# A hybrid decoder layer on one core: the delta rule's outputs split where they are made and loaded as two operands, the second merge's first two tiles in chunk order, the mixer's last pair at a lower priority

## The chip, the core and the metric

One Trainium2 chip, one of its cores. The metric is the device time of one execution in microseconds, as the median of the runs. TensorE is called PE here, VectorE DVE, ScalarE ACT, GpSimd POOL, and SyncE SP; nearly all transfers are issued from SP's queue.

## What is computed

One layer for 1024 prompt tokens and 32 sample tokens, width 1024, in float32. Two branches read the same normalised input: stick-breaking attention (8 heads of 64) and a gated delta rule (4 heads of 128). They are merged through two gates and two projections, and a channel mixer follows:

```python
q_a, k_a, v_a, u, z, a, b, g_a, g_b = jnp.split(rmsnorm(x) @ w_in, ...)
o_a = sb_prompt(q_a, k_a, v_a, sb_bias)                    # stick-breaking attention
o_b, ssm_new = gdn_branch(short_conv(u), z, a, b, ...)     # gated delta rule, chunk by chunk
y_a, y_b = o_a @ w_pa, o_b @ w_pb
x = x + (sigmoid(g_a) * y_a + sigmoid(g_b) * y_b) @ w_o
x = x + square(relu(rmsnorm(x) @ w_up)) @ w_down
```

## The kernel before

Every dense product is made of three. A float32 operand is split into a rounded part `h` (an ACT copy into the type F32R) and the rest `l` (a DVE subtraction), and `dense()` (lines 134 to 139) adds `wh·xh`, `wh·xl` and `wl·xh` over the contraction's tiles into one PSUM bank. Each operand of PE must therefore exist as two tiles.

The order of instructions on each engine's queue is not written out by hand. It is laid down when the kernel is built, by a planner that gives each engine, among what it holds to be ready, the instruction with the highest priority. Priority is the place in the program; `tc.high_priority()` puts a block at the very front, `high_priority(offset=n)` moves it forward by `n` places (a negative `n` moves it back), and `tc.issue_after(x)` keeps a block's instructions behind `x` on the queue. On the chip each queue runs in that order, whatever is ready.

The work goes in stages. `gdn_head(h)` (head of the delta rule, four calls) makes one head's output: after the last chunk it loads the gate `z_d[h]` into `zl`, a tile of the tag "cgb" (one buffer, shared with `qe` of the next head), multiplies it with the transposed output (L585) and stores it from SP to `o_d[4 + h]` (L586). The tag "vb" (one buffer) holds `vb`, the scaled values of a head, which the chunk loop's first product reads (L551). The sample tokens' output `dot` is stored in the same way (L778).

From about 640 us to 850 us the attention's 64 blocks (`blks`) run through a pipeline. For each block PE makes scores, ACT the sigmoid, POOL the mask and `1 - s` (L961, L964), DVE a running product and a multiplication (L968, L969), PE transposes (L111) and the products with the values (L1006, L1020). `pipeline(x0, x1, fill)` spreads other work for PE between the blocks. For the blocks up to 34 that is the gates' projections (`pd_g`, stores L1073); for the blocks from 34 on it is the second merge's `o_B @ w_pb`: 32 steps `pb_step(j, c, first)`, one for each of 8 column tiles `j` and 4 token chunks `c` (256, 256, 256 and 288 tokens). A step is `dense4` of 12 matmuls on `obh[c]`, `obl[c]`, and a product with the stored gate `tb[j]` on DVE (L1174). The steps go tile by tile, so that the fourth step needs the fourth chunk.

Between the two parts of the pipeline the input's pools are closed (`xctx`) and others opened in their place: `tbp` for the gates, `z2p`, and `obp` for `obh`, `obl` and one of the staging tiles. The delta rule's outputs come in here. Chunk 0 was loaded ahead at L1111 into a tile `ofb0` of a pool that was already there; chunks 1 to 3 are loaded at L1153 into `z2p` and `obp`. ACT copies each chunk into `obh[c]` (L1155), and DVE subtracts into `obl[c]` (L1156), both under `high_priority()`. `mark` is the last of these loads, and the gates of the tiles from 2 on are loaded behind it (L1169).

The mixer's first stage works on pairs of row tiles. `up_products(w7, f, g)` makes seven products, combines them on DVE, takes relu and square of two pairs of rows on ACT (L1437, L1438), combines those on DVE in `combos` (L1364 to L1367) and stores the result from SP into `hc_d` (L1368). Its last call is `(f, g) = (15, 1)`. The second stage begins at once: its loads are issued from POOL (L1495, L1503), `weight_part` splits the weights on ACT and DVE (L1517, L1518; the first part under `high_priority()`), and `pw` is its first product. The result of the last pair is read only in the last of three groups of that stage.

## Time and profile before

| | us |
|---|---|
| median of 3 runs | 1700.03 |
| lowest and highest run | 1699.78, 1703.91 |
| the profiled execution | 1701.33 |
| its span, first to last instruction | 1699.6 |

The profile is of one execution. Its span is 1.7 us shorter than that execution's own time. Of the span, PE is busy 98%, DVE 69%, ACT 46% and POOL 13%. The page's chain of work gives 89% of the span to PE, 4% to DVE, 2% to DMA, and 1% each to POOL and ACT. To read it: idle time of PE is what can be saved, in the stage where it stands, and the rows say what ended it; a busy PE runs at the granted clock, which is 1.00 in most stretches and lower in a few.

### The profile page before, as it was taken

How to read it: one execution, taken by the hardware profiler on the slowest of the kernel's cores; microseconds unless marked ns; L12 is line 12 of the kernel's file. 1: busy time of each engine (PE TensorE's matmuls, PEld its weight loads, DVE VectorE, ACT ScalarE, POOL GpSimd, SP SyncE). 2: the span in 40 equal slices, each digit the busy share in tenths (PEclk: the TensorE clock that was granted, in tenths of full speed). 3: DMA queues.
4: the chain of work that ended last, by engine and by line, in shares of the span. 5: the costliest groups of instructions: out<-in, count | busy, mean ns of one | idle time of the engine just before them, and what ended most of it. 6: DMA issues, size and time to landing. Idle time of an engine off the chain costs nothing.

```text
span 1699.6 us, 34650 instructions
## 1 busy us (share of the span) xinstructions
PE 1665.5 (98%) x13934; PEld 1616.3 (95%) x13934; DVE 1170.7 (69%) x2335; ACT 778.5 (46%) x1548; POOL 220.7 (13%) x243
## 2 busy tenths in 40 slices
PE   7999999999999999999999999999999999999998
PEld 6999999999999799988999999999999999999998
DVE  6656676877325337789776578877777678688964
ACT  5453434343324225555433455644444564334455
POOL 1110111110004226565300000000000000000000
PEclk9999999999999999999999999999999999999999
DMA  5132233244538577895144545555443765442231
GB/s 182 38 119 81 70 95 104 74 124 129 159 90 240 156 194 180 203 237 178 42 130 144 166 134 159 155 161 162 140 140 117 270 210 190 151 158 97 96 114 78
DMA packets 260205, 240.86 MB, mean 142 GB/s; under 512 B 55906, under 2 KB 217795, under 8 KB 260044
## 3 DMA queue, kind: packets, MB, share of 16 engines
q1 hardware_dynamic: 255094, 227.90, 44.4%
q0 software_dynamic: 3200, 10.52, 2.1%
q8 instruction: 109, 1.79, 0.4%
q10 hardware_dynamic: 1750, 0.23, 0.1%
q14 instruction: 52, 0.43, 0.1%
HBM read 164.02 MB, written 74.58 MB: 140 GB/s over the span
## 4 chain that ended last, share of the span: by engine, by line
PE 89%; DVE 4%; issue 2%; DMA 2%; POOL 1%; ACT 1%; SPq 0%; DVEq 0%; POOLq 0%; ACTq 0%
PE pu L139 6%; PE pu L137 6%; PE pu L138 6%; PE pw L137 6%; PE pw L138 6%; PE pw L139 6%; PE pd_g L137 3%; PE pd_g L138 3%; PE pd_g L139 3%; PE wt L111 1%; PE px L138 1%; PE px L137 1%; PE px L139 1%; PE pd_uk L139 1%; PE po L1006 1%
## 5 line engine op out<-in xcount | busy, mean ns | idle before, releaser
L137 PE MATMUL pu<-Xh,uh 128*128 128x264 f32 x812 | 229.8, 284 | 0.5 <-ACT t L1426 0.5
L139 PE MATMUL pu<-Xh,ul 128*128 128x264 f32 x812 | 230.1, 285 | 0.0
L138 PE MATMUL pu<-Xl,uh 128*128 128x264 f32 x812 | 229.8, 283 | 0.0
L137 PE MATMUL pw<-hc,w 128*128 128x264 f32 x784 | 220.8, 285 | 2.8 <-ACT w L1517 2.4
L138 PE MATMUL pw<-hc,w 128*128 128x264 f32 x784 | 220.0, 286 | 0.0
L139 PE MATMUL pw<-hc,w 128*128 128x264 f32 x784 | 216.3, 286 | 0.0
L137 PEld LDWEIGHTS pu<-Xh,uh 128*128 128x128 f32 x812 | 153.2, 189 | 0.9 <-ACT t L1426 0.7
L138 PEld LDWEIGHTS pu<-Xl,uh 128*128 128x128 f32 x812 | 152.8, 188 | 0.0
L139 PEld LDWEIGHTS pu<-Xh,ul 128*128 128x128 f32 x812 | 152.1, 188 | 0.0
L137 PEld LDWEIGHTS pw<-hc,w 128*128 128x128 f32 x784 | 148.1, 189 | 3.2 <-ACT w L1517 2.6
L137 PE MATMUL pd_g<-xh,wh_g 128*128 128x256 f32 (+1 forms) x512 | 149.9, 293 | 0.0
L138 PE MATMUL pd_g<-xl,wh_g 128*128 128x256 f32 (+1 forms) x512 | 149.6, 292 | 0.0
L139 PE MATMUL pd_g<-xh,wl_g 128*128 128x256 f32 (+1 forms) x512 | 149.0, 291 | 0.0
L138 PEld LDWEIGHTS pw<-hc,w 128*128 128x128 f32 x784 | 147.1, 189 | 0.0
L139 PEld LDWEIGHTS pw<-hc,w 128*128 128x128 f32 x784 | 145.7, 190 | 0.0
L968 DVE TENSOR_TENSOR_SCAN pr<-am 128x127 f32<-128x127 f32 (+7 forms) x64 | 89.5, 1399 | 19.1 <-POOL am L964 15.7
L137 PEld LDWEIGHTS pd_g<-xh,wh_g 128*128 128x128 f32 x512 | 97.2, 190 | 3.2 <-issue 2.6
L138 PEld LDWEIGHTS pd_g<-xl,wh_g 128*128 128x128 f32 x512 | 97.3, 190 | 2.5 <-issue 2.1
L139 PEld LDWEIGHTS pd_g<-xh,wl_g 128*128 128x128 f32 x512 | 97.1, 190 | 2.1 <-issue 2.0
L1517 ACT ACTIVATE w<-a 128x512 fp32r<-128x512 f32 x84 | 46.6, 620 | 94.6 <-PE pw L139 88.2
L1490 ACT ACTIVATE hc<-hc 128x528 fp32r<-128x528 f32 x98 | 62.1, 644 | 28.8 <-DMA hc<-hc_d 26.8
L139 PE MATMUL px<-mh,wl_wo 128*128 128x264 f32 x256 | 72.5, 286 | 1.3 <-DVE wl_wo L1262 1.2
(582 smaller groups left out, 5014.8 us busy)
## 6 DMA issues: line engine op xcount, KB each, us to landing
hc_d<-t SPq DMA_DIRECT2D x27, 924.0 KB
hc<-hc_d SPq DMA_DIRECT2D x94, 264.0 KB
a<-in_w_down_dram SPq DMA_DIRECT2D x52, 256.0 KB
ws_c<-in_w_in_dram SPq DMA_DIRECT2D x16, 512.0 KB
ws_wo<-in_w_o_dram SPq DMA_DIRECT2D x32, 256.0 KB
ua<-in_w_up_dram SPq DMA_DIRECT2D x16, 512.0 KB
ub<-in_w_up_dram SPq DMA_DIRECT2D x16, 512.0 KB
gA_d<-gt SPq DMA_DIRECT2D x8, 528.0 KB
```

The lines of the kernel that those rows point to most:

```text
L111: return PE.transpose(out, in_, ident[:k, :k])
L137: PE.matmul(pt[:, :n], lhsT=wh[k], rhs=xh[k], start=(k == 0), stop=False)
L138: PE.matmul(pt[:, :n], lhsT=wh[k], rhs=xl[k], start=False, stop=False)
L139: PE.matmul(pt[:, :n], lhsT=wl[k], rhs=xh[k], start=False, stop=(k == nk - 1))
L968: V.tensor_tensor_scan(pr[:, n - 1:0:-1], am_r, am_r, 1.0, op0=ALU.mult, op1=ALU.bypass)
L1006: PE.matmul(po[64 * r:64 * r + 64, 0:P], lhsT=vn[:, b, rs], rhs=wts[hh, 2 * m + r][:, b * P:(b + 1) * P], start=(b == 0), stop=(b == 2 * m ...
L1490: S_.activation(tl[:, 0], tl[:, 1].bitcast(F32), AF.Copy)
L1517: S_.activation(tl[:, 0], src, AF.Copy)
```

## The change

Three edits. First, `gdn_head` splits its output where it is made: ACT copies `zl` into a new tile `zh` (tag "vb"), DVE subtracts, and two stores replace the one, into two new buffers `ob_d`. The same goes for the sample tokens' `dot` (its copy takes a buffer of the tag "dyt"). In the merge the four chunks of `obh` and `obl` are then loaded directly, eight loads from SP in place of four loads, four ACT copies and four DVE subtractions; the load ahead at L1111 and the staging tiles fall away, and the first two gates' loads stand behind chunk 0's.

Second, the first eight steps of `pb_step` go chunk by chunk over the tiles 0 and 1; the other 24 stay as they were.

Third, relu, square, combinations and store of the pair (15, 1) stand under `high_priority(offset=-600)`, 600 places further back.

```diff
--- before.py
+++ after.py
@@ -146,6 +146,7 @@
     xT_d, o_d, x1_d = spill("xT_d"), spill("o_d"), spill("x1_d")
     gA_d, gB_d = spill("gA_d"), spill("gB_d")
     z_d = dr.tile([GH, P, NP], F32, name="z_d")
+    ob_d = [dr.tile([GH, P, T], F32, name=f"ob{x}_d") for x in "hl"]
     q_d = [dr.tile([4, P, NP], F32, name=f"q{x}_d") for x in "hl"]
     k_d = [dr.tile([4, P, NP], F32, name=f"k{x}_d") for x in "hl"]
     v_d = dr.tile([4, P, NC, P], F32, name="v_d")
@@ -583,7 +584,11 @@
         for hf, pt in enumerate(tr8(on, f"o{h}", gtile)):
             sl = slice(hf * 512, hf * 512 + 512)
             V.scalar_tensor_tensor(zl[:, sl], zl[:, sl], gnw, pt, op0=ALU.mult, op1=ALU.mult)
-        SY.dma_start(o_d[4 + h, :, 0:NP], zl)
+        zh = gk.tile([P, NP], F32R, tag="vb", name=f"zh{h}")
+        S_.activation(zh, zl, AF.Copy)
+        V.tensor_tensor(zl, zl, zh.bitcast(F32), op=ALU.subtract)
+        SY.dma_start(ob_d[0][h, :, 0:NP], zh.bitcast(F32))
+        SY.dma_start(ob_d[1][h, :, 0:NP], zl)
 
     for h in range(GH):
         gdn_head(h)
@@ -775,7 +780,11 @@
     dot = dk.tile([P, GH, NS], F32, name="dot")
     V.scalar_tensor_tensor(dot.rearrange("p h c -> p (h c)"), zs.rearrange("p h c -> p (h c)"), gnw, pot[:, 0:P],
                            op0=ALU.mult, op1=ALU.mult)
-    SY.dma_start(o_d[4:8, :, NP:T].rearrange("h p c -> p h c"), dot)
+    doh = dk.tile([P, GH, NS], F32R, tag="dyt", name="doh", bufs=2)
+    S_.activation(doh, dot, AF.Copy)
+    V.tensor_tensor(dot, dot, doh.bitcast(F32), op=ALU.subtract)
+    for dst, src in zip(ob_d, (doh.bitcast(F32), dot)):
+        SY.dma_start(dst[:, :, NP:T].rearrange("h p c -> p h c"), src)
     dkp = dk.tile([P, P], F32, name="dkp")
     V.tensor_scalar(dkp, knd, degc, None, op0=ALU.mult)
     vexp = dk.tile([P, NSEQ, P], F32, tag="big", name="vexp")
@@ -1107,8 +1116,6 @@
             if t % 2 == 1 and t >= 3:
                 fills.append(lambda t=(t - 3) // 2: residual_step(t))
     pipeline(0, SPLIT, fills)
-    ofb0 = zp.tile([P, 4, 256], F32, tag="zz", name="ofb0")
-    SY.dma_start(ofb0, o_d[4:8, :, 0:256].rearrange("k p c -> p k c"))
     xctx.close()
     tbctx = ExitStack()
     oa3 = pool("oa3", stack=tbctx)
@@ -1141,20 +1148,9 @@
     for c in range(len(CX)):
         ob_tiles(c)
     for c, (o, n) in enumerate(CX):
+        for dst, src in zip((obh[c], obl[c]), ob_d):
+            mark = SY.dma_start(dst.bitcast(F32), src[:, :, o:o + n].rearrange("k p c -> p k c"))
         if c == 0:
-            st = ofb0
-        else:
-            if c == 1:
-                st = z2p.tile([P, 4, 288], F32, tag="zz", name="ofb1")[:, :, 0:256]
-            elif c == 2:
-                st = obp.tile([P, 4, 256], F32, name="ofb2")
-            else:
-                st = z2p.tile([P, 4, 288], F32, tag="zz", name="ofb3")
-            mark = SY.dma_start(st, o_d[4:8, :, o:o + n].rearrange("k p c -> p k c"))
-        with tc.high_priority():
-            S_.activation(obh[c], st, AF.Copy)
-            V.tensor_tensor(obl[c], st, obh[c].bitcast(F32), op=ALU.subtract)
-        if c == 2:
             for j in range(2):
                 SY.dma_start(tbs[j], gB_d[j])
     wbs = {}
@@ -1173,7 +1169,9 @@
         with tc.high_priority():
             V.tensor_tensor(tb[:, o:o + n], pt[:, :n], tb[:, o:o + n], op=ALU.mult)
 
-    steps = [lambda j=j, c=c, f=(x == 0): pb_step(j, c, f) for j in range(KT) for x, c in enumerate(range(4))]
+
+    order = [(j, c) for c in range(4) for j in range(2)] + [(j, c) for j in range(2, KT) for c in range(4)]
+    steps = [lambda j=j, c=c: pb_step(j, c, c == 0) for j, c in order]
     pipeline(SPLIT, NB - 2, steps[:-6])
     pipeline(NB - 2, NB, steps[-6:])
     ofa = []
@@ -1433,13 +1431,15 @@
             V.tensor_tensor(t[:, 1], u2, p4, op=ALU.subtract)
             V.tensor_tensor(t[:, 3], p3, u1, op=ALU.add)
         rows = (t[:, 0:4:3], t[:, 1:7:5])
-        for r in range(2):
-            S_.activation(rows[r], rows[r], AF.Relu)
-            S_.activation(rows[r], rows[r], AF.Square)
-            if f < NPL:
-                SY.dma_start(by_group(h_d[f + NF * r], g), rows[r])
-        if f >= NPL:
-            combos(f, g, t)
+
+        with tc.high_priority(offset=-600) if (f, g) == (NF - 1, 1) else ExitStack():
+            for r in range(2):
+                S_.activation(rows[r], rows[r], AF.Relu)
+                S_.activation(rows[r], rows[r], AF.Square)
+                if f < NPL:
+                    SY.dma_start(by_group(h_d[f + NF * r], g), rows[r])
+            if f >= NPL:
+                combos(f, g, t)
 
     out_proj(0)
     blocks(0)
```

## Rows read from the trace of the kernel before

**Rows 1.** The head of the page and its first part: busy time of an engine, its share of the span, its instructions.

```profile
span 1699.6 us, 34650 instructions
...
PE 1665.5 (98%) x13934; PEld 1616.3 (95%) x13934; DVE 1170.7 (69%) x2335; ACT 778.5 (46%) x1548; POOL 220.7 (13%) x243
```

**Rows 2.** The windows view over the stage where the attention pipeline runs beside the `o_B @ w_pb` products, in three stretches: the stretch, its length, busy us (and instructions) of PE, PE's weight loads, DVE, ACT and POOL, then granted clock, DMA share, GB/s.

```profile
710.00:760.00 50.00, 47.71 (x414) 42.64 (x413) 41.67 (x39) 29.99 (x65) 28.77 (x32) 0.99 0.90 223
760.00:800.00 40.00, 38.31 (x302) 32.79 (x301) 37.95 (x38) 19.98 (x39) 23.14 (x20) 0.97 0.76 220
800.00:850.00 50.00, 50.00 (x464) 45.77 (x462) 36.60 (x51) 24.23 (x52) 18.05 (x26) 1.00 0.13 37
```

**Rows 3.** The waits view for PE from 700 to 870 us: who waited for whom, us in total, times, the longest.

```profile
PE pb L138 <- DVE obl L1156: 2.7, 2, 2.1
PE pb L137 <- DVE tb L1174: 1.0, 2, 0.8
...
PE pb L137 <- ACT obh L1155: 0.2, 1, 0.2
```

**Rows 4.** The windows view in stretches of 4 us around the start of those products (columns as in Rows 2).

```profile
748.00:752.00 4.00, 4.00 (x26) 2.90 (x24) 1.64 (x1) 3.33 (x9) 2.60 (x3) 1.00 0.97 316
...
756.00:760.00 4.00, 1.94 (x12) 1.94 (x13) 4.00 (x4) 0.93 (x4) 3.91 (x4) 0.85 1.07 280
760.00:764.00 4.00, 4.00 (x23) 3.62 (x22) 4.00 (x4) 1.56 (x3) 3.74 (x4) 0.72 1.10 264
```

**Rows 5.** The timeline of PE at the first product of the second merge: start, us, line, output and inputs, form, in brackets the idle time before it and what ended it.

```profile
755.07 0.38 PE L137 MATMUL pb<-obh,wh_pb 128*128 128x256 f32 x1 [0.16 <-ACT obh L1155]
...
758.06 0.38 PE L138 MATMUL pb<-obl,wh_pb 128*128 128x256 f32 x1 [2.11 <-DVE obl L1156]
```

**Rows 6.** The timeline of DVE there (the two outputs' splits L1156, beside a multiplication of the attention's chain).

```profile
756.02 1.99 DVE L1156 TENSOR_TENSOR obl<-ofb,obh 128x1024 fp32r<-128x1024 f32 x1
757.93 1.17 DVE L969 TENSOR_TENSOR s<-s,pr 128x895 f32<-128x895 f32 x1
759.02 1.30 DVE L1156 TENSOR_TENSOR obl<-ofb,obh 128x1024 fp32r<-128x1024 f32 x1
```

**Rows 7.** The timeline of ACT there: the splits L1155 and the last idle time before them.

```profile
751.38 1.27 ACT L960 ACTIVATE s<-sc,sbb 128x512 f32<-128x512 f32 x2 [0.38 <-issue]
...
753.01 2.01 ACT L1155 ACTIVATE obh<-ofb 128x1024 fp32r<-128x1024 f32 x2
```

**Rows 8.** The tile view of `obh`: duration in ns (least, median, most) of the splits, first and last start, forms.

```profile
L1155 ACT ACTIVATE obh<-ofb x4: 1048/1064/1163, 753.0 to 770.9; 128x1024 fp32r<-128x1024 f32 x3, 128x1152 fp32r<-128x1152 f32 x1
L1156 DVE TENSOR_TENSOR obl<-ofb,obh x4: 1304/1808/2087, 756.0 to 775.4; 128x1024 fp32r<-128x1024 f32 x3, 128x1152 fp32r<-128x1152 f32 x1
```

**Rows 9.** The timeline of SP's DMA queue, the loads and stores on which the next part rests (the duration is that of the issue, not of the transfer).

```profile
648.29 0.39 SPq L1111 DMA_DIRECT2D ofb<-o_d  x1
...
748.08 0.76 SPq L123 DMA_DIRECT2D ws_pb<-in_w_pb_dram  x1
...
752.14 0.53 SPq L878 DMA_DIRECT2D qs<-qh_d  x1
753.50 0.38 SPq L1153 DMA_DIRECT2D ofb<-o_d  x1
754.73 0.44 SPq L878 DMA_DIRECT2D kl<-kl_d  x1
...
758.02 0.60 SPq L878 DMA_DIRECT2D kl<-kl_d  x1
```

**Rows 10.** The waits view of SP's DMA queue from 744 to 766 us.

```profile
SPq L878 <- DMA ws_pb<-in_w_pb_dram: 1.0, 1, 1.0
```

**Rows 11.** The timeline of DVE at the tail of DeltaNet head 0: `zl` (L585), the next head's work and the wait for `cgb` (L491).

```profile
255.51 1.55 DVE L585 SCALAR_TENSOR_TENSOR zl<-zl,vec,t_o 128x512 f32<-128x512 f32 x2 [0.94 <-PE t_o L111]
263.30 0.87 DVE L510 TENSOR_SCALAR U<-l 32x256 f32<-32x256 f32 x2 [6.24 <-PE l L508]
...
265.78 1.23 DVE L491 TENSOR_TENSOR cgb<-cvq,cgb 128x1024 f32<-128x1024 f32 x1 [1.15 <-ACT cgb L490]
...
268.03 1.22 DVE L128 TENSOR_TENSOR wl_uq<-ws_uq,wh_uq 128x1024 fp32r<-128x1024 f32 x1
```

**Rows 12.** The timeline of SP there: the store of `zl` (L586) and the load that takes over its buffer (L489).

```profile
257.09 0.32 SPq L586 DMA_DIRECT2D o_d<-zl  x1
259.72 0.32 SPq L489 DMA_DIRECT2D cgb<-cg_d  x1
```

**Rows 13.** The timeline of PE at the seam between the mixer's two stages (L139 `pu` is the last product of the last pair, L137 `pw` the first of the next stage).

```profile
1344.59 0.39 PE L137 MATMUL pw<-hc,w 128*128 128x264 f32 x1 [2.40 <-ACT w L1517]
...
1347.20 1.96 PE L139 MATMUL pw<-hc,w 128*128 128x264 f32 x8
```

**Rows 14.** The windows view over the half-clock stretch there (columns as in Rows 2).

```profile
1340.00:1350.00 10.00, 7.61 (x51) 7.40 (x50) 6.84 (x15) 8.06 (x15) 0.00 (x0) 0.83 0.99 335
```

**Rows 15.** The timeline of ACT there: relu and square of the last pair (L1437, L1438), the weights' splits (L1517).

```profile
1341.24 0.65 ACT L1437 ACTIVATE t<-t 128x528 f32<-128x528 f32 x1 [4.20 <-DVE t L1433]
...
1343.93 1.13 ACT L1517 ACTIVATE w<-a 128x512 fp32r<-128x512 f32 x2
```

**Rows 16.** The timeline of DVE there: the first of the four combinations (L1364 to L1367) and the weights' splits (L1518).

```profile
1344.05 0.43 DVE L1364 TENSOR_TENSOR t<-t 128x264 f32<-128x264 f32 x1 [1.38 <-ACT t L1438]
...
1345.68 1.29 DVE L1518 TENSOR_TENSOR w<-a,w 128x512 fp32r<-128x512 f32 x2
```

## What I expect, and why

> **What bounds the kernel now.** I read the page first, then the windows by stage, PE's waits, and the timelines of single engines at the two places that the change touches. PE is busy in 1665.5 of 1699.6 us [rows 1]. The work of PE is the same after the change: the same matmuls on the same operands. What can be won is therefore PE's idle time in the stages touched, and time at the lower clock. The reader should see how little that is.
>
> In the merge's stage PE is busy 47.71 of 50 us and 38.31 of 40 us, while DVE is busy 41.67 and 37.95: DVE is the engine that others wait for. From 800 us on PE is busy throughout [rows 2]. The waits of that stage that belong to `pb` are 2.7 us for `obl`, 1.0 us for `tb` and 0.2 us for `obh` [rows 3]. Most of it is one gap: PE stops at 755.95 and goes on at 758.06, when the first `obl` is there [rows 5]. It came late because DVE made it from 756.02 on, in 1.99 us [rows 6]. Right behind the gap the granted clock falls: 0.85 and 0.72 as means of two stretches of 4 us, which is 1.2 in place of 2.4 GHz for part of each [rows 4]. PE had been busy 1.94 of 4 us there. The loss is (0.15 + 0.28) × 4 = 1.7 us.
>
> At the seam in the mixer PE waits 2.40 us for the first weights' split [rows 13]; then the clock is at 0.83 over 10 us [rows 14], another 1.7 us. So the most that the three edits could return is about 3.9 + 1.7 + 2.4 + 1.7 = 9.7 us, or 0.6%.
>
> **First edit, in the heads.** Each head gains an ACT copy of 128x1024 (1.06 us, as L1155 has for this form [rows 8]), a DVE subtraction (1.22 us, as L128 [rows 11]), and one more issue on SP (0.32 us [rows 12]). Four heads: 4.2 us of ACT, 4.9 us of DVE. PE doesn't read any of it here. After `zl` of head 0 DVE stands idle for 6.24 us [rows 11], which covers the subtraction; if it weren't there, the next head's operations would come 1.22 us later.
>
> Two buffers are held longer. The tag "cgb" is free when `zl` has been stored. Before, the store is issued at 257.09 and the next load into the buffer at 259.72 [rows 12]. Now copy and subtraction come first, 1.06 + 1.22 = 2.3 us. DVE waits 1.15 us for that buffer's successor as it is, and the weights' split `wl_uq` for PE stands behind that wait [rows 11]. With the order unchanged, three heads would each lose up to 2.3 us on DVE, and PE some part of it: 0 to 6.9 us. The order is laid down anew, however, with the longer hold known to the planner, and the wait that remains is what the planner doesn't foresee of two transfers, which stay two. I take 0.4 us in all, near the lower end, because the rows show free DVE time in front of the wait. The tag "vb" is now held by `zh` until its store lands, some 5 us after `zl`; the next head's values come later by that, and are first read when its chunk loop starts. I put that at nothing; the cover is the solve and projections in between. The sample tokens' part is small and far from any reader.
>
> **First edit, in the merge.** It takes away four ACT copies (1.06 us each) and four DVE subtractions (median 1.8 us [rows 8]), 7 us of DVE in the stretch where DVE is fullest. It puts transfers in their place: eight loads of 512 or 576 KB, 4.3 MB, where 1.6 MB were loaded in the stage and 0.5 MB ahead of it at 648.29 [rows 9].
>
> When do they start? Both operands now lie in `obp`, from their load on. Before, ACT first wrote into that pool at 753.01, though chunk 0 had been issued at 648.29, though the copies have the highest priority, and though ACT had just had an idle time [rows 7, 9]. So the pool isn't to be had earlier: it lies where the last gate's tile lies. On SP the first load into it stands behind `qs` of 752.14, at 753.50 [rows 9]. I take 753 for the first issue.
>
> When do they land? A load of the same 512 KB and the same row length, `ws_pb`, was issued at 748.08, and SP waited for it before an issue at 754.73 [rows 9, 10]: up to 6.6 us, with DMA at 0.97 to 1.10 of its capacity [rows 4]. Then `obl[0]`, second in the queue, is there at about 759.7, which is later than DVE's 758.06.
>
> The Trainium skill ("DMA: Bandwidth & Descriptors", Anatomy of one DMA) gives a fixed cost of about 2 us and then bytes at 436 GB/s; by that both operands of chunk 0 would be there some 4.4 us after the issue, at about 757.4, and the gap would shrink. The stage's rows show 264 to 316 GB/s and the longer landing, so the sum goes by them.
>
> The wait at the first product: before 0.16 + 2.11 = 2.3 us. After, it lies between 0.5 us (DVE is free of the 1.99 us, so the attention's chain moves up and its transposes fill PE) and 759.7 − 755.95 = 3.7 us (the queue stands behind the product). I take 2.0, in the middle: a gain of 0.3 us. The later waits for `obl`, 2.7 − 2.1 = 0.6 us, go. Those for `tb`, 1.0 us, are DVE's lateness, and I let half go. The clock's 1.7 us I leave, since a gap of like length remains; it could also go, or come twice. Sum for the merge: −0.3 − 0.6 − 0.5 = −1.4 us, between −5.6 (all of 2.3 + 0.6 + 1.0 + 1.7) and about +3.
>
> Who else is moved? The remaining loads of head 6's `qs`, `kh`, `kl`, the last at 758.02 [rows 9], come behind the eight, and land later by 3.7 MB at some 0.3 MB/us, 12 us. Their scores are two rounds of blocks away, so I put that at nothing; without that distance it would cost the whole 12 us.
>
> **Second edit.** Two tiles on chunk 0, then two on chunk 1: the fourth chunk is needed by the seventh step and not the fourth. The work is the same. A step is 12 matmuls at 50/464 = 0.11 us [rows 2], 1.3 us, so each chunk's loads, 1.05 MB or 3.3 to 4.0 us at the rates above, have 2.6 us of products and the attention's work beside them. That just covers it; with the old order it wouldn't. I put it at nothing by itself.
>
> **Third edit.** The idea would be that the weights' split no longer waits behind the last relu and square. ACT stands idle for 4.20 us before the first of them, and the split comes right after the last, at 1343.93 [rows 15]. But that split already has the highest priority there is. If the planner had held it to be ready in those 4.20 us, it would stand there now. On DVE all four combinations (from 1344.05) stand ahead of the first weights' subtraction (1345.68) [rows 16], which has the front's priority as well: for the planner the weights come later still. Moving the relus back gives way to something that isn't there. So the order of ACT should stay, and the 2.40 us with it. The store into `hc_d` may fall behind the next loads and let them land earlier, but PE hardly waits for those. I take −0.4 us, between 0 and −4.1 (2.4 and 1.7).
>
> **The sum.** +0.4 − 1.4 − 0.4 = −1.4 us. The profiled execution would go from 1701.33 to 1699.9, and the median, which stands 1.3 us below that execution, from 1700.03 to 1698.6.
>
> **The rivals.**
> - A, the loads land in time. The waits at `pb` and the fall of the clock go: −5.6 + 0.4 − 0.4 = −5.6, 1694.4. For it: SP could be free for them a few us earlier, and DVE and POOL are relieved. Against it: the 6.6 us of `ws_pb`. The Trainium skill's page "DMA: Bandwidth & Descriptors" (Anatomy of one DMA) points this way, by its landing at 757.4.
> - B, the last pair does make room: −4.1 in place of −0.4, so 1694.9. For it: the ACT row, if the planner's view of readiness is not as I read it. Against it: the priorities above.
> - A and B together: 0.4 − 5.6 − 4.1 = −9.3, 1690.7.
> - C, slower: PE's queue stands behind the loads. If the planner takes the eight loads to be faster than they are, it puts products ahead of the attention's work, and PE stops for each chunk: 3.7 − 2.3 = 1.4 us more at the first, then 4.0 − 2.6 = 1.4 us at three more, and the clock once more, 1.7: with the 0.6 and 0.5 us gained, about +6.2, 1706.2. It decides from the point at which `obl[0]` lands after 758.06. For it: DMA is full there [rows 4]. Against it: PE has the attention's work to do meanwhile.
> - D, slower: "cgb" is late in three heads, 6.9 us in place of 0.4: 1705.1. Against it: the planner knows the longer hold.
>
> **How the numbers follow.** The measurement can tell 0.3%, 5.1 us, from no change: faster is below 1694.9, slower above 1705.1. Chances: forecast 0.55, A 0.16, B 0.10, both 0.05, C 0.08, D 0.06. Faster: two thirds of A, half of B (they stand at the limit), and both, 0.21, with a little of the forecast's edge 0.22. Slower: half of C and of D, and an edge, 0.08. The rest, 0.70, is within. The range is 1693.5 to 1704.0: it takes in the forecast, A and B, and leaves out A and B together, C and D, 0.19.
>
> **What would show it.** Heads: PE's idle time from 170 to 480 us is as before within 1 us; D would show as longer waits for `cgb` and `wl_u`. Merge: the first `pb` with `obl` near 759 to 760, waiting for a DMA; A would show it before 757 and no stretch below 1.00. DVE's busy time there falls by some 7 us. Seam: the wait for L1517 is still near 2.4 us; B would have the splits ahead of L1437 on ACT. I am wrong if PE's work itself costs otherwise, or if the new order moves waits in stages that the change doesn't touch.

## The result, and the profile after

| | us |
|---|---|
| median before, 6 runs beside the changed kernel's | 1701.13 |
| median after, 6 runs | 1708.97 |
| ratio, with its 95% interval | 1.0049 (1.0030 to 1.0069) |
| profiled execution after, and its span | 1709.9, 1708.2 |

The changed kernel is slower by half a per cent. The forecast was 1698.6 us, the range ended at 1704.0, and slower had a chance of 0.08. On two other chips the ratio was 1.0054 (1.0037 to 1.0072) and 1.0037 (1.0022 to 1.0052).

The head of the page and its first part, after:

```profile
span 1708.2 us, 34702 instructions
...
PE 1666.2 (98%) x13934; PEld 1617.5 (95%) x13934; DVE 1166.4 (68%) x2336; ACT 778.6 (46%) x1549; POOL 224.2 (13%) x243
```

Against [rows 1] PE's work is the same, 1666.2 against 1665.5 us; the span grew by 8.6 us, so PE's idle time grew by 7.9. The windows view says where. Before, over four stages (columns as in Rows 2):

```profile
170.00:480.00 310.00, 306.25 (x2745) 300.58 (x2744) 205.35 (x527) 122.77 (x305) 31.90 (x28) 1.00 0.36 107
640.00:700.00 60.00, 60.00 (x523) 55.55 (x522) 45.38 (x40) 33.29 (x72) 33.92 (x34) 1.00 0.74 174
700.00:885.00 185.00, 179.83 (x1474) 162.55 (x1474) 151.08 (x179) 93.49 (x193) 75.86 (x83) 0.99 0.58 160
1340.00:1352.00 12.00, 9.61 (x67) 9.40 (x66) 8.84 (x18) 9.10 (x16) 0.00 (x0) 0.86 1.00 344
```

After, over the same stages (the last one's edges are moved by the shift of 8.7 us):

```profile
170.00:480.00 310.00, 303.43 (x2715) 298.18 (x2715) 206.50 (x527) 125.51 (x305) 31.67 (x28) 0.99 0.37 112
640.00:700.00 60.00, 56.48 (x466) 51.96 (x464) 46.36 (x42) 30.45 (x68) 34.78 (x37) 0.97 0.81 180
700.00:885.00 185.00, 179.58 (x1511) 162.62 (x1510) 142.02 (x167) 92.62 (x197) 83.28 (x87) 1.00 0.64 173
1348.70:1360.70 12.00, 9.60 (x67) 9.40 (x66) 7.87 (x16) 8.31 (x15) 0.00 (x0) 0.86 1.03 353
```

Length minus PE's busy time is the idle time: 3.75 becomes 6.57 us in the heads (170 to 480), 0 becomes 3.52 (640 to 700), 5.17 becomes 5.42 in the merge (700 to 885), and the seam keeps its 2.4 us. Two places carry 6.3 of the 7.9 us: one that the prediction priced at 0.4 us, and one that it didn't price.

**The heads.** PE's waits from 160 to 480 us; before, the largest was 1.7 us for `ntk` (two waits) and the one for `U` came to 0.4:

```profile
PE l L504 <- DVE U L495: 2.0, 2, 1.4
PE t_nv L111 <- ACT ntv L838: 1.1, 2, 0.9
PE pd_av L137 <- DVE ksT L832: 0.8, 1, 0.8
```

They are short, and spread over places that the edit doesn't name. The timeline of DVE at the tail of head 2 (the third head) shows what stands between (L589 is the new subtraction, L495 makes `U`, for which PE waited 1.44 us here, L128 splits weights for PE, and PE waited 0.80 us for the `ksT` behind it):

```profile
433.69 1.25 DVE L495 STREAM_TRANSPOSE U<-t 128x1024 f32<-128x1024 f32 x1 [1.95 <-DMA t<-tv_d]
434.86 1.18 DVE L589 TENSOR_TENSOR zl<-zl,zh 128x1024 f32<-128x1024 f32 x1
435.96 1.22 DVE L128 TENSOR_TENSOR wl_g<-ws_c,wh_g 128x1024 fp32r<-128x1024 f32 x1
437.09 0.18 DVE L832 COPY ksT<-pd_ak 128x32 f32<-128x32 f32 x1
437.19 1.28 DVE L487 TENSOR_TENSOR vb<-t_v,s 128x512 f32<-128x512 f32 x2
```

Before, the scaling `vb<-t_v` (L486) stood ahead of that tail, at 421.54 and 423.51 us. Now (L487) it stands behind the subtraction, since its buffer is `zh`'s until `zh` is read and stored. PE waits nowhere for `vb` itself. Behind two gaps near 347 us (0.59 and 0.85 us) the granted clock is low as well, which costs (1 − 0.79) × 8 = 1.7 us (windows view):

```profile
348.00:356.00 8.00, 7.43 (x84) 7.02 (x85) 4.29 (x9) 3.24 (x8) 0.00 (x0) 0.79 0.88 282
```

Rival D's sign is there too: DVE waits twice as long for `cgb` in the heads, before and after (waits view of DVE, 160 to 520 us):

```profile
DVE cgb L491 <- ACT cgb L490: 5.7, 3, 2.6
DVE cgb L492 <- ACT cgb L491: 11.5, 2, 7.6
```

PE hardly feels it: behind the longest of these waits, which ends at 449.64 us, PE stops once, for 0.16 us.

**Near 654 us.** This stage holds none of the edited lines. PE stops once, for 3.5 us, for the attention's sigmoid (L969), because ACT stood before it for 8.07 us for the gate's weights. ACT's timeline, and then SP's:

```profile
655.57 1.06 ACT L127 ACTIVATE wh_g<-ws_c 128x1024 fp32r<-128x1024 f32 x1 [8.07 <-DMA ws_c<-in_w_in_dram]
...
656.82 1.15 ACT L969 ACTIVATE s<-sc,sbb 128x512 f32<-128x512 f32 x2
```

```profile
623.23 0.36 SPq L945 DMA_DIRECT2D o_d<-osT  x1
...
632.95 0.45 SPq L887 DMA_DIRECT2D qs<-qh_d  x1
...
640.79 0.33 SPq L996 DMA_DIRECT2D vn<-v_d  x1
643.25 0.33 SPq L1082 DMA_DIRECT2D gA_d<-gt  x1
644.44 0.38 SPq L237 DMA_DIRECT2D ws_c<-in_w_in_dram  x1
```

The load of `ws_c` stands behind seven loads for the attention and a store, and ACT had it 11.1 us after its issue. The same seven loads and the store stood ahead of it before; what moved is the time. SP and ACT, before:

```profile
616.37 0.36 SPq L936 DMA_DIRECT2D o_d<-osT  x1
...
635.89 0.38 SPq L236 DMA_DIRECT2D ws_c<-in_w_in_dram  x1
```

```profile
649.41 1.06 ACT L127 ACTIVATE wh_g<-ws_c 128x1024 fp32r<-128x1024 f32 x1
```

SP stands until DVE has made `osT`, the sample tokens' attention output, and issues its store 6.9 us later than before. From the issue of `ws_c` to ACT's need of it there were 13.5 us before, and now there are 3.1 (ACT is free for it at 647.50). In the new order, then, ACT and PE come to this place early and SP comes late. After the gap the clock falls there too (windows view); this stretch is the third place of the loss:

```profile
656.00:664.00 8.00, 6.44 (x38) 5.95 (x38) 7.69 (x6) 5.17 (x12) 5.39 (x4) 0.79 0.94 206
```

**The merge.** The first product with `obl`, its load and SP's waits of 700 to 725 us, after (timelines of PE and SP, waits of SP, and the landing in the tile view of `obl`, which the trace has for the third chunk's load alone, issued at 769.85):

```profile
768.16 0.95 PE L111 MATMUL wt<-ident,s 128*128 128x128 f32 x7 [1.29 <-DVE s L978]
...
775.71 0.38 PE L138 MATMUL pb<-obl,wh_pb 128*128 128x256 f32 x1
```

```profile
707.49 1.29 SPq L1020 DMA_DIRECT2D o_d<-oT  x2
713.28 0.33 SPq L1180 DMA_DIRECT2D ofa<-o_d  x1
...
763.71 0.60 SPq L1152 DMA_DIRECT2D obh<-obh_d  x1
764.36 0.53 SPq L1152 DMA_DIRECT2D obl<-obl_d  x1
```

```profile
SPq L1180 <- DMA o_d<-oT: 4.4, 1, 4.4
```

```profile
DMA to landing us min/median/max: 10.1/10.1/10.1
```

The loads start at 763.71, 10.2 us behind the 753.50 of before; the stages ahead had cost about as much by then (2.8 and 1.7 in the heads, 0.6 from 480 to 640 us, 3.5 and 1.7 near 654 us). The one `obl` whose landing the trace has took 10.1 us, not 6.6. The landing of `obl[0]` isn't recorded; it was there at the latest 11.4 us after its issue, since PE doesn't wait for it at 775.71. PE does the attention's work first, and waits for that (1.29 us at 768.16). What the edit didn't name is the load `ofa` at 713.28. Taking `ofb0` away emptied its buffer (tag "zz"); the next tenant, attention output `ofa0`, was loaded at 758.72 before, and now at 713.28, where SP stands 4.4 us for the store of `o_d` to land, with all later loads behind it.

**The seam.** PE's and ACT's rows, against [rows 13, 15]: the same wait, the same order.

```profile
1353.30 0.39 PE L137 MATMUL pw<-hc,w 128*128 128x264 f32 x1 [2.40 <-ACT w L1517]
```

```profile
1352.63 1.13 ACT L1517 ACTIVATE w<-a 128x512 fp32r<-128x512 f32 x2
```

### The profile page after: what moved, and what is told of

It is laid out like the page before. It is cut to its first block, busy times and chain, and to the rows that moved or that the text cites. A ratio compares the mean times of both kernels' runs of the same rounds, so it can differ in the third digit from the quotient of the medians.

```text
span 1708.2 us, 34702 instructions
## 1 busy us (share of the span) xinstructions
PE 1666.2 (98%) x13934; PEld 1617.5 (95%) x13934; DVE 1166.4 (68%) x2336; ACT 778.6 (46%) x1549; POOL 224.2 (13%) x243
## 4 chain that ended last, share of the span: by engine, by line
PE 83%; DMA 6%; DVE 5%; issue 3%; ACT 1%; SPq 1%; POOL 0%; DVEq 0%; POOLq 0%; ACTq 0%
PE pu L139 6%; PE pu L137 6%; PE pu L138 6%; PE pw L138 5%; PE pw L139 5%; PE pw L137 5%; PE pd_g L137 3%; PE pd_g L139 3%; PE pd_g L138 3%; PE wt L111 2%; PE po L1015 1%; PE px L138 1%; PE px L139 1%; PE px L137 1%; PE pd_z L137 1%
## 5 line engine op out<-in xcount | busy, mean ns | idle before, releaser
L139 PE MATMUL pu<-Xh,ul 128*128 128x264 f32 x812 | 229.9, 284 | 0.0
L137 PE MATMUL pu<-Xh,uh 128*128 128x264 f32 x812 | 229.6, 283 | 0.2 <-ACT t L1424 0.2
L137 PE MATMUL pw<-hc,w 128*128 128x264 f32 x784 | 220.7, 285 | 2.5 <-ACT w L1517 2.4
L139 PE MATMUL pw<-hc,w 128*128 128x264 f32 x784 | 216.3, 285 | 0.2 <-DVE w L1518 0.2
L137 PEld LDWEIGHTS pu<-Xh,uh 128*128 128x128 f32 x812 | 153.1, 189 | 0.6 <-ACT t L1424 0.4
L139 PEld LDWEIGHTS pu<-Xh,ul 128*128 128x128 f32 x812 | 152.0, 188 | 0.0
L137 PEld LDWEIGHTS pw<-hc,w 128*128 128x128 f32 x784 | 148.0, 189 | 2.9 <-ACT w L1517 2.6
L137 PE MATMUL pd_g<-xh,wh_g 128*128 128x256 f32 (+1 forms) x512 | 149.9, 293 | 0.2 <-ACT gt L1077 0.2
L139 PE MATMUL pd_g<-xh,wl_g 128*128 128x256 f32 (+1 forms) x512 | 149.2, 291 | 0.0
L139 PEld LDWEIGHTS pw<-hc,w 128*128 128x128 f32 x784 | 145.5, 189 | 0.4 <-DVE w L1518 0.4
L137 PEld LDWEIGHTS pd_g<-xh,wh_g 128*128 128x128 f32 x512 | 97.5, 190 | 3.3 <-issue 2.4
L139 PEld LDWEIGHTS pd_g<-xh,wl_g 128*128 128x128 f32 x512 | 97.3, 190 | 2.8 <-issue 2.4
L1517 ACT ACTIVATE w<-a 128x512 fp32r<-128x512 f32 x84 | 46.7, 620 | 96.8 <-PE pw L139 88.3
L973 POOL TENSOR_SCALAR am<-s 128x128 f32<-128x128 f32 (+7 forms) x64 | 77.5, 1211 | 6.7 <-DVE pr L977 1.4
```

The source lines that it names most:

```text
L137: PE.matmul(pt[:, :n], lhsT=wh[k], rhs=xh[k], start=(k == 0), stop=False)
L139: PE.matmul(pt[:, :n], lhsT=wl[k], rhs=xh[k], start=False, stop=(k == nk - 1))
L973: G.tensor_scalar(am[:, :n], s[:, :n], -1.0, 1.0, op0=ALU.mult, op1=ALU.add)
L1517: S_.activation(tl[:, 0], src, AF.Copy)
```

## Experiments

Each set ran on one chip, and the kernel before ran beside it. Chips differ (medians of 1701.5 to 1710.4 us for it), so the verdicts go by the ratio, with its 95% interval; a difference in us is (ratio − 1) times the kernel before's median. The table gives PE's idle time in one profiled execution each, as length minus PE's busy time in three windows; the reader should look down its columns, and within a set. From 480 to 640 us, which it leaves out, PE's idle time goes with the chip: 3.8 to 5.6 us in every kernel of sets 1 and 2, 2.9 in set 5, and under 1 us in the first two traces and in sets 3 and 4 (e3_work 2.2). e1_seam, with PE's order as before, has 4.70 there against 0.

```
                        170-480  640-700  700-885   ratio
before                    3.75     0.00     5.17
changed kernel            6.57     3.52     5.42    1.0049
set 1  e1_seam            3.92     0.00     6.74    1.0000
       e1_heads           6.09     0.60     6.69    1.0036
       e1_merge           3.74     0.00     9.35    1.0024
       e2_nw              8.77     0.96     6.05    1.0068
set 2  e2_after           6.04     1.65     7.14    1.0054
       e2_hold            6.35     0.00     6.69    1.0014
       e2_mload           4.40     0.00    11.96    1.0049
       e2_late            4.10     0.32     9.07    1.0024
set 3  e3_work            5.45     0.00     5.29    1.0011
       e3_ofa             6.43     1.90     5.63    1.0021
       e3_lateofa         3.95     1.47     5.36    0.9997
       e3_mix             3.60     0.93     5.83    0.9993
set 4  e4_after           6.26     1.30     7.78    1.0037
       e4_ofa             6.10     1.55     5.06    1.0038
       e4_fetch           5.93     0.00     8.58    1.0040
       e4_both            6.49     0.00     5.14    1.0020
set 5  e5_mixxl           3.74     1.05     6.56    1.0016
       e5_ordxl           3.97     0.00     6.55    1.0007
```

### The three edits, one at a time

The heads alone:

```diff
+        zh = gk.tile([P, NP], F32R, tag="vb", name=f"zh{h}")
+        S_.activation(zh, zl, AF.Copy)
+        V.tensor_tensor(zl, zl, zh.bitcast(F32), op=ALU.subtract)
+        SY.dma_start(ob_d[0][h, :, 0:NP], zh.bitcast(F32))
+        SY.dma_start(ob_d[1][h, :, 0:NP], zl)
...
-            mark = SY.dma_start(st, o_d[4:8, :, o:o + n].rearrange("k p c -> p k c"))
+            mark = SY.dma_start(st, ob_d[0][:, :, o:o + n].rearrange("k p c -> p k c"))
```

> Only the first edit's part in the heads and the sample tokens: split, two stores. The second merge loads and splits as in the kernel before, but from the rounded part alone, so its operand lacks the low part. Theory T (the split in the heads re-lays the queues, and the loss lies ahead of the merge): 7 to 11 us slower than before, PE idle 6 to 7 us between 170 and 480 us, and the 3.5 us wait near 654 us is there again; the merge keeps its 2.1 us wait for obl. Rival R1 (the eight loads in the merge cost the time): within 2 us of before.

1716.49 against 1710.44 us: 1.0036 (1.0021 to 1.0051), +6.2 us, a little less than expected, and the wait near 654 us is 0.60 us, not 3.5. This edit alone costs about as much as the smallest of the whole change's three losses (6.3 us, in set 4). Idle time is only a part of it: against e1_seam on the same chip the profiled span is 5.8 us longer (1714.5 against 1708.7), of which PE's idle time is 1.7 and PE's busy time 4.1 (1669.0 against 1664.9). What lengthens the busy time isn't shown.

The merge alone, eight loads and the new order:

```diff
+        for dst, src in zip((obh[c], obl[c]), (o_d[4:8], o_d[4:8])):
+            mark = SY.dma_start(dst.bitcast(F32), src[:, :, o:o + n].rearrange("k p c -> p k c"))
...
+    order = [(j, c) for c in range(4) for j in range(2)] + [(j, c) for j in range(2, KT) for c in range(4)]
```

> Only the merge: eight loads in place of four with their copies and subtractions, and the second edit's order; the heads store as before, and both operands are read from that one buffer, so the low operand holds the whole value. Theory T: 1 to 4 us faster than before, since the 2.1 us wait at the first products and the half clock behind it go, and some waits for the attention's multiplication come; nothing near 654 us. Rival R1 (the loads cost the time): 5 us or more slower, with PE waiting for the loads.

1714.84: 1.0024 (1.0011 to 1.0037), +4.1 us, where −1.4 was forecast; neither theory had this. PE's waits from 700 to 885 us in it:

```profile
PE sc L958 <- ACT s L960: 3.3, 2, 2.5
PE wt L111 <- DVE s L969: 2.7, 2, 1.6
```

The waits for `obl` are gone; those for the attention's `s` have come in their place. None of PE's is for the loads themselves, as R1 would have it.

The last pair alone:

```diff
+        with tc.high_priority(offset=-600) if (f, g) == (NF - 1, 1) else ExitStack():
```

> Only the third edit, relu, square, combinations and store of the last pair 600 places back. Theory T: the queues stay as they were, so no change, within 1 us of before, and the wait for L1517 at the seam is 2.40 us. Rival B of the prediction: 4 us faster, the split of the weights ahead of the relus on ACT. Rival R2 (it disturbs the second stage's start): 2 us or more slower.

1710.51: 1.0000 (0.9989 to 1.0011); the wait for L1517 is there with 2.39 us.

### What in the heads costs

The whole change, with the rounded part in another tag:

```diff
-        zh = gk.tile([P, NP], F32R, tag="vb", name=f"zh{h}")
+        zh = gk.tile([P, NP], F32R, tag="nw", name=f"zh{h}")
```

> All three edits, but the heads' rounded part takes the buffer of the tag nw (the normalised output, whose last reader is the transposition just before) in place of the tag vb. Theory T1 (the hold of vb, which puts the next head's scaled values behind the split, is what re-lays the heads): PE idle between 170 and 480 us back at 3.5 to 4.5 us, no half clock there, and the time 4 to 10 us below the changed kernel, 1699 to 1705. Rival T2 (the added copy, subtraction and store re-lay them by themselves): 1706 to 1710, with PE idle of 6 us or more there.

1721.73: 1.0068 (1.0049 to 1.0086), +11.6 us, more than with "vb", and outside both expectations. So the hold of "vb" is not the one trigger: without it the loss is larger (though the buffer of "nw" is held in its place). Here rival D's mechanism reaches PE: DVE waits 7.92 us for `cgb`, and PE 3.09 us for the `U` that DVE makes behind it (timelines of DVE and PE).

```profile
453.48 1.22 DVE L492 TENSOR_TENSOR cgb<-cvq,cgb 128x1024 f32<-128x1024 f32 x1 [7.92 <-ACT cgb L491]
...
455.21 0.94 PE L543 MATMUL wt<-U,kb 128*128 128x128 f32 x4 [3.09 <-DVE U L535]
```

The kernel before, with the hold and nearly none of the work:

```diff
+        zh = gk.tile([P, NP], F32R, tag="vb", name=f"zh{h}")
+        S_.activation(zh[:, 0:1], zl[:, 0:1], AF.Copy)
+        SY.dma_start(ob_d[0][h, :, 0:1], zh[:, 0:1].bitcast(F32))
```

> The kernel before, with a tile of the tag vb at the end of each head into which ACT copies one column and which one small store reads; the whole output is stored as before and no other part of the change is in. Theory T1 (holding vb over the end of a head re-lays the heads): most of the heads' loss without the added work, 3 us or more slower than before. Rival T2 (the added copy, subtraction and second store do it): within 2 us of before.

1711.15 against 1708.84: 1.0014 (1.0000 to 1.0027), +2.4 us, between the two expectations.

The kernel before, with the work and no hold or store:

```diff
         SY.dma_start(o_d[4 + h, :, 0:NP], zl)
+        S_.activation(on, zl, AF.Copy)
+        V.tensor_tensor(on, on, zl, op=ALU.subtract)
```

> The kernel before, with an ACT copy of 128x1024 and a DVE subtraction of 128x1024 at the end of each head behind the store, written over the normalised output (whose values nobody reads any more); no new tile, no second store, the results are used by nothing. Theory T2 (the added operations alone re-lay the heads): 3 us or more slower than before, with PE idle of 5 us or more between 170 and 480 us. Rival T4 (it takes the holds of buffers to do it): within 2 us of before.

1705.56 against 1701.89: 1.0011 (0.9994 to 1.0028), +1.9 us, an interval that reaches both expectations. In the table either of the two, hold or work, already brings most of the idle time of the whole split (6.35 and 5.45 against 5.93 to 6.57 us; 3.60 to 4.40 where the heads' tails are as before). They don't add up, and each alone makes the planner lay the queues down anew: PE's 13934 matmuls in order of time (output and inputs, without buffer numbers), set beside those of the kernel before line by line, differ in 806 lines in e1_heads, in 870 in e2_hold, in 312 in e3_work, and in none in e1_seam. How much of the order changes is not a measure of the time lost.

The whole change, with the split moved out of the heads: `o_d` is stored as before, and reloaded, split and stored behind the sample tokens' part:

```diff
+    for h in range(GH):
+        zr = lk.tile([P, NP], F32, tag="zr", name=f"zr{h}")
+        SY.dma_start(zr, o_d[4 + h, :, 0:NP])
+        zh = lk.tile([P, NP], F32R, tag="zh", name=f"zh{h}")
+        S_.activation(zh, zr, AF.Copy)
+        V.tensor_tensor(zr, zr, zh.bitcast(F32), op=ALU.subtract)
```

> All three edits, but the prompt's outputs are stored whole in the heads, as before, and loaded again, split and stored as two operands behind the sample tokens' part, near 520 to 600 us, where DVE and ACT stand idle more than half of the time. Theory T (the split in the heads is what costs there): heads as before, PE idle of 3.8 us between 170 and 480 us, and 3 to 6 us less than the changed kernel. Rival T3 (more work anywhere ahead of the merge re-lays as much): no better than the changed kernel.

1711.62: 1.0024 (1.0011 to 1.0037). The heads' idle time is back at 4.10 us, and the kernel is 5.1 us faster than the whole change on that chip (1711.62 against 1716.67), though it does more work. The theory's forecast holds. It stands where the merge alone stood.

### The order of the steps

The eight loads with the old order:

```diff
-    order = [(j, c) for c in range(4) for j in range(2)] + [(j, c) for j in range(2, KT) for c in range(4)]
+    steps = [lambda j=j, c=c, f=(x == 0): pb_step(j, c, f) for j in range(KT) for x, c in enumerate(range(4))]
```

> The merge's eight loads alone, in the old order of the steps; heads as before, both operands read from the one buffer, so the low operand holds the whole value. Theory M1 (the loads cost what the splits gave, whatever the order of the steps): 2 to 6 us slower than before, as with the second edit. Rival M2 (the second edit's order is what costs): within 1 us of before or faster. By the prediction's own step (the fourth chunk is needed by the fourth step) it would be slower than with the new order, by 1 to 4 us.

1717.51: 1.0049 (1.0026 to 1.0071), +8.4 us against e1_merge's +4.1 on another chip. The intervals overlap, but the idle time points the same way (11.96 against 9.35 us), and so do the waits:

```profile
PE pb L137 <- DVE tb L1161: 5.1, 6, 2.2
PE sc L958 <- ACT s L960: 3.6, 2, 3.2
```

The whole change, for the interval on this chip:

> The changed kernel itself, as the measure for the others of this set. Theory T (the loss lies ahead of the merge, by a new order in the heads and by transfers there): 5 to 10 us slower than before; PE idle between 170 and 480 us again near 6.6 us against 3.8. Rival R3 (the single 3.5 us wait near 654 us is the larger half of the loss): it is there again; if the loss is there without that wait, R3 falls.

1716.67: 1.0054 (1.0037 to 1.0072). PE's idle time near 654 us is 1.65 us here, so that wait is not the larger half of the loss, as R3 had it.

### The load that moved ahead

`ofa0` and `ofa1` kept behind the merge's loads, in the whole change (e3_ofa, e4_ofa) and in e2_late (e3_lateofa):

```diff
-        SY.dma_start(st, o_d[k])
+        with tc.issue_after(mark.ins):
+            SY.dma_start(st, o_d[k])
```

> The changed kernel, with the load of ofa0 kept behind the eight chunk loads on SP. That load takes the buffer in which chunk 0 was staged ahead, so without the staging it is issued some 50 us earlier, where SP stops for a store of the same buffer to land. Theory M3 (that stop puts all later loads back, so that ACT waits for the weights ws_pb and for ofs, and PE for ACT): ACT's waits for these two fall below 1 us each, PE's wait for the scores near 760 us goes, and the kernel is 2 to 4 us faster than the changed one (5 to 7 us above before). Rival M4 (the loss in the merge is the lost load ahead of chunk 0, since products can't begin before the loads land): within 1.5 us of the changed kernel, 8 to 10 us above before.

> The kernel with the splits behind the sample tokens' part (which stood 4 us above before), and with ofa0's load behind the chunk loads. Theory M3: 1 to 3 us above before or less. Rival M4: still 3 to 5 us above, with PE's waits for the attention's transposes (wt for s, 4.8 us) unchanged.

1707.47 and 1703.24 against 1701.89: 1.0021 (1.0002 to 1.0039) and 0.9997 (0.9979 to 1.0016). With the splits out of the heads and this load held back, nothing measurable of the loss is left; the interval reaches 2.7 us above before.

> The changed kernel again, as the measure on the chip of this set: 7 to 10 us above before, with the heads' six waits, a wait for the scores near 655 us and waits in the merge.

> The changed kernel with ofa0's load behind the chunk loads, now on the same chip as the changed kernel. Theory M3: 3 to 5 us below the changed kernel, no wait of ACT for ws_pb or ofs over 1 us. Rival M6 (its gain in the last set came from another chip): within 1.5 us of the changed kernel.

On one chip with each other the two gave 1708.36 and 1707.36, against 1701.54: 1.0037 and 1.0038 (1.0025 to 1.0052). That is no gain that can be measured, as rival M6 had it, though the waits changed as expected. PE's waits from 700 to 885 us, first with the load ahead (e4_after), then with it behind (e4_ofa):

```profile
PE wt L111 <- DVE s L978: 3.8, 2, 2.1
PE sc L967 <- ACT s L969: 1.0, 1, 1.0
```

```profile
PE wt L111 <- DVE s L978: 2.3, 2, 1.3
PE pb L137 <- DVE tb L1170: 1.3, 2, 0.8
```

### The weights behind the attention's loads

Head 2's loads kept behind the gate's weights (`gate_loads` is the list of these loads), alone and with the edit above:

```diff
+            with tc.issue_after(gate_loads[13].ins) if hh == 2 else ExitStack():
+                heads[hh] = attn_load(hh)
```

> The changed kernel with the loads of the attention's head 2 (qs, kh, kl and the values vn) kept on SP behind the load of the next gate's weights; PE, ACT and POOL keep their order. Theory G (the wait for the scores near 655 us comes from that weights' load, which lies on SP behind 3 MB of the attention's loads; ACT waits for it and PE for ACT): that wait goes, ACT waits under 1 us for ws_c there, and the kernel is 1 to 5 us below the changed one. Rival G2 (the DMA engines are full anyway, so what is put back is as late): the wait moves to the scores of head 2, no gain.

> Both together: ofa0's load and head 2's loads put back. Theories M3 and G: the gains add, 2 to 4 us above before is left, which is the heads' share. If G falls: as with ofa0 alone.

1708.75, 1.0040 (1.0023 to 1.0057), and 1704.64, 1.0020 (1.0005 to 1.0034). SP now has `ws_c` ahead, and from 640 to 700 us PE's idle time is 0:

```profile
635.15 0.38 SPq L237 DMA_DIRECT2D ws_c<-in_w_in_dram  x1
635.59 1.93 SPq L887 DMA_DIRECT2D qs<-qh_d  x1
```

Alone it gained nothing: the merge had 8.58 us of idle time in place of 7.78. Together the two took 2.9 of the 6.3 us that the ratio of e4_after stands for; the two intervals still overlap. The median of e4_both lies 2.7 to 4.1 us below those of the three others on its chip, a gain that neither edit shows alone.

### A version that might beat both

e2_late with chunk 0 loaded ahead and split in the merge, as before, and chunks 1 to 3 as pairs; then that with the products on the low part last, for the first two tiles; then the kernel before with the new order and the low part last:

```diff
+                S_.activation(obh[0], ofb0, AF.Copy)
+                V.tensor_tensor(obl[0], ofb0, obh[0].bitcast(F32), op=ALU.subtract)
...
+            prods = [(a[k], obh[c][:, k]) for k in range(4) for a in (wh, wl)] + [(wh[k], obl[c][:, k]) for k in range(4)]
```

> As the one with the splits behind the sample tokens' part, but chunk 0 is again loaded ahead whole and split in the merge; chunks 1 to 3 come as two operands, in the new order of steps. Theories M3 and M4 both: the 2.1 us wait for the first obl comes back, those for the later obl don't, the waits for wt and for the scores go; 0 to 3 us faster than before. Rival M5 (six loads of operands load the queue as much as eight): 3 us or more above before.

> The version with late splits and chunk 0 loaded ahead, and in the first eight steps of the merge the four products with the low operand come last, so that 8 products of the rounded one (0.9 us, 1.8 us for two tiles) stand before the first that needs obl. Theory F (what the merge lacks is ready work for PE at its start, not DVE's time): the first wait for obl falls from 1.6 us to below 0.5 us, and the kernel is 1 to 4 us faster than before. Rival F2 (DVE's chain sets the stage whatever PE's order is): the idle time comes back as waits for wt or tb, within 1.5 us of before.

> The kernel before with its own loads and splits, the second edit's order of steps, and in the first eight steps the products with the low operand last. Theory F: the 2.1 us wait for the first obl falls below 0.5 us and the half clock behind it goes, 1 to 4 us faster than before. Rival F2: within 1.5 us of before, with waits for wt or tb in its place.

1703.44 against 1701.89, 0.9993 (0.9977 to 1.0008); 1711.41 against 1709.07, 1.0016 (0.9997 to 1.0035); 1709.82, 1.0007 (0.9993 to 1.0022). None beats the kernel before. In e5_mixxl PE's wait for `obl` is gone, and waits of 2.5 us for `tb` at these products and 2.1 us for `kh` stand there: the wait that theory F names goes, but its gain doesn't come. In e5_ordxl the wait for `obl` falls from 2.7 us [rows 3] to 1.0, not below 0.5, and others come up (PE's waits):

```profile
PE sc L958 <- DMA kh<-kh_d: 1.5, 1, 1.5
PE pb L1177 <- DVE tb L1181: 1.2, 1, 1.2
```

## Why the prediction was wrong

**Right.** PE is the bound, and there was at most 9.7 us to win. The seam kept its order and its wait, and its edit measured 1.0000. DVE's busy time in the merge fell by 9.1 us, for a forecast of some 7 (151.08 to 142.02). The old order of the steps had more idle time (e2_mload), though the times' intervals overlap. Head 6's last load was issued at 778.90, some 11 us later if the 10.2 us by which everything stands later there are taken off, for a forecast of 12, and PE didn't wait for it. That the loads land late while DMA is full was right in kind, and too short in size: 512 KB took 10.1 us where the landing is recorded (obl of the third chunk, DMA share 1.10 from 769 to 781 us), more than the rows' bound of 6.6. The Trainium skill ("DMA: Bandwidth & Descriptors", Anatomy of one DMA) gave an estimate of 4.4 for both parts of the chunk; its fit is for single transfers issued from GpSimd, and these were issued from SP behind others.

**The step that failed first** is the heads: "I take 0.4 us in all, near the lower end, because the rows show free DVE time in front of the wait", and for "vb", "I put that at nothing". Measured: +2.8 us of idle time and 1.7 us of clock in the first trace, +6.2 us for the edit alone, 5.1 us by moving the split out. The free time was real, but it was read in an order that the change abolishes. The tails of the heads are woven from the next head's scaling, the solve, and the attention's projections on four queues; a new tenant of "vb" and two more instructions re-lay all of that, and PE's small waits stand in the new order. That they come from it is the reading of the traces, not shown by itself. That the order is laid anew was even an argument of the prediction, but only for a smaller cost. The upper bound of 6.9 us had the right size by luck. Its mechanism, the wait for `cgb`, did come, and on DVE it nearly reached that size: 5.7 us of waiting became 11.5. But the kernel's loss isn't this wait: PE stopped 0.16 us behind it in the changed kernel, and 3.09 us only in e2_nw. How the cost divides between hold, work and stores stays open: hold and work alone measured +2.4 and +1.9 us, with intervals that reach no change.

**The second step** is the merge, "−1.4 us". In the first trace it came to about that: +0.25 of idle time, and 1.7 us of clock less, since the low stretch of [rows 4] is gone; but by other items, and not by a rule: e2_after, the same kernel, has a clock of 0.79 over 764 to 772 us and again over 774 to 782. The first product with `obl` came at 775.71, about 766 on before's clock (less the 10.2 us) and not 759.7, and waits for the attention's `s` replaced those for `obl`. On other chips it cost: +4.1 us alone. The list of what the edit takes away had the loads, copies and subtractions, but not the buffer that comes free, whose next tenant is now loaded 45 us earlier by the traces' times and stops SP. In set 4 the merge's idle time is 7.78 and 8.58 us with that load early and 5.06 and 5.14 with it held back; in sets 1 and 2 it is 9.35 and 9.07 (e1_merge, e2_late) where kernels with the old merge have 6.7. But e2_after (7.14) and the first trace (5.42) show little of it. The time followed in e4_both against e4_fetch (1704.64 against 1708.75) and, over two chips, in e3_lateofa against e2_late; it did not in e4_ofa against e4_after. That this load stops SP, and in set 4 makes PE wait, is shown; what it costs in time isn't settled.

**Not in the sum** were the 3.5 us near 654, and the low clock behind them. Moving loads on SP removes the wait (e4_fetch), so that queue makes it: SP stands longer for `osT` and issues `ws_c` late. This stop is 16.6 to 20.9 us in e1_heads and in the changed kernel's three traces, where ACT then waits 4.9 to 8.1 us for `ws_c`, and 9.5 to 10.7 us in the kernels without any split ahead of the merge, where ACT doesn't wait for this load. In the table this stage's idle time is 0 in every kernel without the split and 0.32 to 3.52 us in those with it, but for the two that moved the loads; the same kernel shows 3.52, 1.65 and 1.30. (In e2_nw, e2_late and the versions built on e2_late ACT doesn't wait for this load, so their idle time there has another origin.) Removing it bought no time by itself. The prediction's last sentence named the case, "moves waits in stages that the change doesn't touch", and gave it no chance; the 0.14 of C and D stood for mechanisms that didn't decide here, though D's showed on DVE.

## What to carry to other kernels

Where a planner lays the queues down, price an edit by who shares its buffers, not only by its instructions: list for each tile added or removed the tenant before and after it, and what that tenant's load will then wait for. Work put "in free time" is free only in the order that one reads; here four small splits in it cost 6.2 us, for a forecast of 0.4. The same splits placed where nobody waits made the changed kernel 5.1 us faster (e2_late), with more work. An engine that waits longer is no loss yet: DVE's wait for `cgb` doubled and PE hardly felt it, so a rival has to name the wait of the engine that bounds the kernel.

## What the runs showed of the hardware

The same wait at the seam is followed by the low clock in some executions and not in others: PE busy 7.61 of 10 us both times, granted clock 0.83 in e4_ofa and 1.00 in e1_merge (windows view, one row each).

```profile
1345.00:1355.00 10.00, 7.61 (x50) 7.40 (x50) 7.81 (x15) 8.45 (x16) 0.00 (x0) 0.83 1.01 351
```

```profile
1352.00:1362.00 10.00, 7.61 (x63) 7.40 (x62) 7.61 (x15) 8.67 (x16) 0.00 (x0) 1.00 1.01 348
```

So the 1.7 us that the prediction counted there are not a fixed part of the kernel. The same holds for the 1.7 us near 350 us: in e4_after, the same kernel, the clock is 1.00 from 344 to 356 us behind gaps of 0.83 and 0.61 us. And a DMA share above 1 doesn't say how much is moved: at 1.04 it was 207 GB/s while mostly the attention's loads ran, into 64 partitions in rows of 4 KB, and 376 with the gate's weights, into 128 partitions in rows of 512 bytes (windows view of the changed kernel). Which of the two differences makes it isn't shown.

```profile
631.00:648.00 17.00, 17.00 (x134) 16.74 (x134) 6.81 (x9) 7.29 (x16) 5.90 (x12) 1.00 1.04 207
650.00:652.00 2.00, 2.00 (x18) 1.63 (x17) 0.00 (x0) 0.00 (x0) 0.00 (x0) 1.00 1.04 376
```
